# Hybrid decoder layer: weight splits put 200 places forward in the planner's priorities, and the memory tiles of the values asked for two at a time

## The chip, the cores and the metric

The kernel runs on one core of a Trainium2 chip. A core has a matrix engine (TensorE, PE in the profile; its weight loads are PEld), a vector engine (VectorE, DVE), a scalar engine (ScalarE, ACT), GpSimd (POOL) and a queue engine (SyncE, SP), and 16 DMA engines that all queues share. SBUF is the working memory, PSUM holds the sums that TensorE makes. The metric is the time of one execution in microseconds (us), as the device gives it; the median of three runs is compared.

## The reference

One layer on 512 tokens of width 1024, everything in float32:

```python
x = x + 0.5 * swiglu(rms_norm(x, norm_ffn1_w), ffn1_w_in, ffn1_w_out)        # d_ff 2816
x = x + hybrid_mixer(rms_norm(x, norm_mix_w), ...)    # 16 SSD heads, 8 differential-attention heads
x = x + memory_cross_attention(rms_norm(x, norm_cross_w), rms_norm(mem, norm_mem_w), w_cq, w_ck, w_cv, w_co)
x = x + 0.5 * swiglu(rms_norm(x, norm_ffn2_w), ffn2_w_in, ffn2_w_out)
out = rms_norm(x, norm_final_w)
```

The part that the change touches by name is the values of the cross-attention, `v = rms_norm(mem, norm_mem_w) @ w_cv`, with `mem` of 256 rows of width 1024. The other part, the way a weight is made ready, concerns nearly every matrix between the first feed-forward block and the second.

## The kernel before

**Splits.** A float32 product is made of three fast products: each operand is split into a high part (an ACT copy into a shorter format, `wh`, `hmh`, ...) and a low part (DVE: the operand less the high part, `wl`, `hml`, ...), and TensorE computes high x high, high x low, low x high. `split_into` (L152 to L161) issues the pair, the ACT instruction first and the DVE instruction that needs its result second. For weights, `load_w` (L172 to L181) takes one of six raw buffers (`wr`), asks for it on SP, takes one of three pairs `wh`, `wl`, and splits: 1.06 us on ACT and 1.23 us on DVE for a tile of 128x1024. Weight n + 3 gets the pair of weight n when the last product that reads weight n is done, so at most two weights can be ready ahead of the one that TensorE works on. One weight tile feeds 24 products of 512 columns, 5.4 us of TensorE. The quads of both feed-forward blocks (`raw_w`, `split_w`) and the last matrix (`out_blocks`) have splits of their own, which the change does not touch.

**Who decides the order.** Python generators write the program down in one long list. `Order` keeps a clock `t` that each written matmul moves on by its estimated time (520 columns at 2400 a microsecond, 0.22 us), a list of dense generators (projections) and a list of spawned chains, each with the time at which its next step is due. So the chains' small steps are written between the matmuls of the projections. For SP and POOL the written order is the order of execution (`manual_schedule`). For TensorE, ACT and DVE a planner goes over the list ahead of time: whenever an engine is free in its estimate, it takes the ready instruction with the lowest priority number, and that number is the place in the list. What comes out is one fixed order for each engine; on the chip an engine runs its instructions in this order and waits where an operand is not there. A weight's split is written with its `load_w`, that is when the product before it has been written completely; it gets ahead of work written earlier only where that work is not ready.

**The memory tiles.** `mem` is needed three times: for its norm, for the keys (`hm`) and for the values (`hm2`). `memory_prep` (L966 to L972) asks for the eight tiles of 128x256 at once on SP, with `memory_tile` (L952 to L955), then splits one every 3.0 us of the planner's clock into `hm2` (ACT L159, DVE L160), each placed behind the latest weight's split (`behind(recent)`). The call for the values is in `group_dense(3)` (L813 to L824): the chain starts 1.0 us after the first of the group's four tiles of `wxbc` has begun. A memory tile takes one of 16 small buffers (tag `s1`), which hold the group chains' small tiles (`xde`, `st`) too.

**The surroundings.** `group_dense(g)` makes the four convolved tiles of SSD group g (`xbc_tile`: a projection, then `conv` on ACT L805 and three DVE steps L808, `th` L796 and L797), then two gate tiles (`wz`). The chain `group(g)` (L838 to L947) runs beside the projections that follow: small transposes and products, `st` states (L878 to L886), the decay rows (ACT L899 to L902, DVE L903), `py`, then the norm. `decays` (L829 to L836) brings the decay rows of the next group from DRAM through ACT's own DMA queue into the tiles `gate` and `th` (L835); ACT issues them when the products that read the earlier rows are done. After group 3 come the last three tiles of the attention's output projection (`out_attn`, `pm`, L786), the values of the memory (`memory_values`, `pcv`, weights `wcv`), and the output projection of the SSD part.

Of the kernel before, what the change touches and what calls it, by code (L numbers as in the profile page):

```python
# [20 lines left out]
KT = D // P  # L21
# [18 lines left out]
W |= {"c0": 4.97, "cs": 3.0, "ct": 4.82}  # L40

SPLIT, AHEAD = 5, 2
MASKED = 8e30

B11, B12, B21, B22 = range(4)
# [3 lines left out]
C_FFN1, C_MIX, C_CROSS, C_MEM, C_FFN2, C_SSD = (8 * i for i in range(6))  # L49
# [51 lines left out]
def body(tc, a, dbg=None):  # L101
# [13 lines left out]
    def nm(s):  # L115
        uid[0] += 1
        return f"{s}_{uid[0]}"

    def s2(s, dt=F32, shape=(P, T)):
        if math.prod(shape[1:]) <= T // 2:  # L120
            return sp.tile(list(shape), dt, tag="s1", name=nm(s), bufs=NHALF)
        return sp.tile(list(shape), dt, tag="s2", name=nm(s))
# [7 lines left out]
    def acc(s, shape=(P, T)):  # L130
        return acc_p.tile(list(shape), F32, tag="acc", name=nm(s))
# [10 lines left out]
    od = Order()  # L142
# [9 lines left out]
    def split_into(hi, lo, src, scale=None):  # L152
        if scale is None:
            return (
                S.activation(hi, src, AF.Copy),  # L155
                V.tensor_tensor(lo, src, hi.bitcast(F32), ALU.subtract),  # L156
            )
        return (
            S.activation(hi, src, AF.Copy, scale=scale),  # L159
            V.scalar_tensor_tensor(lo, src, scale, hi.bitcast(F32), ALU.mult, ALU.subtract),  # L160
        )  # L161

    def split(s, src, scale=None, half=False, n=T):
        if half:
            both = s2(s, R32, (P, 2, T // 2))
            hi, lo = both[:, 0], both[:, 1]
        else:
            hi, lo = s2(s + "h", R32, (P, n)), s2(s + "l", R32, (P, n))
        last[:] = [i.ins for i in split_into(hi, lo, src, scale)]
        return hi, lo  # L170

    def load_w(src, n=D):  # L172
        raw = wp.tile([P, n], F32, tag="wr", name=nm("wr"), bufs=6)
        nc.sync.dma_start(raw, src)
        hi = wp.tile([P, n], R32, tag="wh", name=nm("wh"))
        lo = wp.tile([P, n], R32, tag="wl", name=nm("wl"))
        with ExitStack() as after:
            for i in start:
                after.enter_context(tc.issue_after(i))
            recent[:] = [i.ins for i in split_into(hi, lo, raw)]  # L180
        return hi, lo  # L181

    @contextmanager
    def behind(ins):
        with ExitStack() as after:
            for i in ins:
                after.enter_context(tc.issue_after(i))
            yield
# [129 lines left out]
    def proj(ps, w, xs, ks=None):  # L318
        n = len(xs)
        for k in ks or range(n):  # L320
            mm3(ps, w, xs[k], k == 0, k == n - 1, wc=slice(k * P, (k + 1) * P))
            yield


    par = cp.tile([P, NPAR], F32, name="par")
# [154 lines left out]
    def ffn1(h, wa, on_final, at_out):  # L480
        row4, xs = None, []
        wq, plain = iter(a["f1q"]), a["f1i"]
        for ti, (_, nf) in enumerate(THIRDS):
            g = []
            nq = nf // 2
            if ti == 0:
                for made in ffn_first(h, wa):
                    if made is None:
                        yield
                    else:  # L490
                        g.append(split("g", gated(*made, st1.row)))
                row4 = s2("row4")
                V.tensor_scalar(row4, st1.row, 0.5, None, ALU.mult)
                for n in range(NPLAIN - 2):
                    xs.append(block_sums(2 * n, C_FFN1, of_halves(h[2 * n], h[2 * n + 1])))
                    pg, pu = acc("pg"), acc("pu")
                    yield from proj(pg, load_w(plain[n][0]), h)
                    yield from proj(pu, load_w(plain[n][1]), h)
                    g.append(split("g", gated(pg, pu, st1.row)))
                nq -= NPLAIN // 2  # L500
            yield from ffn_quads(xs, wq, st1, nq, whole_tiles(g), BY_TILE)
            at_out(ti)
            for o in range(KT):
                po = acc("po")
                yield from proj(po, load_w(a[f"f1o{ti}"][o], nf * P), g)
                upd = s2("upd")
                V.tensor_tensor(upd, po, row4, ALU.mult)  # L507
                V.tensor_tensor(x[o], x[o], upd, ALU.add)
                if ti == len(THIRDS) - 1:
                    on_final(o)  # L510
# [12 lines left out]
    def beside(ti):  # L523
        if ti == 1:
            od.spawn(prepare())
            od.spawn(memory_norm())
        elif ti == 2:
            od.spawn(memory_prep(hm))
# [17 lines left out]
    def prepare():  # L546
# [19 lines left out]
        rel_far = s2("rel_far", shape=(8, RW - T))  # L566
        V.memset(rel_far, MASKED)
        nc.gpsimd.dma_start(rel_d[:, T:], rel_far)
# [224 lines left out]
    def silu2(src):  # L793

        th = s2("th2")
        S.activation(th, src, AF.Tanh, scale=0.5)  # L796
        V.scalar_tensor_tensor(th, th, 1.0, src, ALU.add, ALU.mult)  # L797
        return th

    def xbc_tile(n, dst):  # L800
        ps = acc("pxbc")
        yield from proj(ps, load_w(a["wxbc"][n]), h)
        y = s2("conv")
        cw = C_CONVW + 4 * n
        S.activation(y, ps, AF.Identity, bias=par[:, C_CONVB + n : C_CONVB + n + 1], scale=par[:, cw + 3 : cw + 4])  # L805
        for j in (2, 1, 0):
            d = 3 - j
            V.scalar_tensor_tensor(y[:, d:], ps[:, : T - d], par[:, cw + j : cw + j + 1], y[:, d:], ALU.mult, ALU.add)  # L808
        dst.append(silu2(y))
# [3 lines left out]
    def group_dense(g):  # L813
        bc, xs, zs = [], [], []
        if g == 3:
            od.spawn(memory_prep(hm2, 3.0), 1.0)
        yield from xbc_tile(8 + g, bc)
        yield from xbc_tile(12 + g, bc)
        for j in range(2):
            yield from xbc_tile(2 * g + j, xs)  # L820
        od.spawn(group(g, bc[0], bc[1], xs, zs), W["g0"])
        for j in range(2):
            ps = acc("pz")
            yield from proj(ps, load_w(a["wz"][2 * g + j]), h)  # L824
            zs.append(silu2(ps))
# [126 lines left out]
    def memory_tile(k):  # L952
        mk = s2("mem", shape=(P, MEM))
        nc.sync.dma_start(mk, a["memT"][k])
        return mk  # L955
# [7 lines left out]
        yield 3.0  # L963
        yield from st_mem.finish(42.0)

    def memory_prep(dst, apart=2.0):  # L966
        mem = [memory_tile(k) for k in range(KT)]
        for k, mk in enumerate(mem):
            with behind(recent):
                dst.append(split("hm", mk, par[:, C_MEM + k : C_MEM + k + 1], True))  # L970
            yield apart

    def memory_keys():
# [67 lines left out]
    hm, hm2 = [], []  # L1041
# [4 lines left out]
    for hd in range(1, 4):  # L1046
        od.add(queries_keys(hd))
    od.add(group_dense(0))
    od.add(out_attn(0, 0, 8))
    od.add(values(1))  # L1050
    for hd in range(4, 8):
        od.add(queries_keys(hd))
    od.add(group_dense(1))
    od.add(out_attn(1, 0, SPLIT))
    od.add(group_dense(2))
    od.add(group_dense(3))
    od.add(out_attn(1, SPLIT, 8, True))
# [352 lines left out]
```

## Time and profile before

| | |
|---|---|
| median of three runs | 1330.36 us (1329.17 to 1332.38) |
| profiled execution | 1330.36 us |
| its span, first to last instruction | 1328.6 us |
| mean granted TensorE clock | 0.995 |
| TensorE busy | 1307.6 us, 98% of the span |
| DVE busy | 946.4 us, 71% |
| ACT busy | 667.5 us, 50% |
| POOL busy | 114.1 us, 9% |

The profile has one row per group of instructions, wait or issue. In a timeline a row has the start and the duration in us from the beginning of the span, the engine (a q behind it marks the engine's queue, which issues transfers), the line of the kernel, the operation, what it writes and reads, the number of merged instructions, and in brackets how long the engine sat idle before it and what ended that. A row of the waits names who waited for whom, with the total, the number of times and the longest. TensorE's matmuls overlap: one that lasts 0.39 us starts 0.23 us after the one before it when TensorE runs freely. So time lost on TensorE is read from the starts: the distance of two starts less 0.23 us.

### The profile page before, as it was taken

Reading aid. Unit: us, or ns where it says so; the run is one execution under the profiler, and the core shown is the slowest. Engines: PE = TensorE matmul, PEld = TensorE weight load, DVE = VectorE, ACT = ScalarE, POOL = GpSimd, SP = SyncE. Lnnn points to the kernel's source line nnn. Section 1 sums busy time; section 2 is a strip of 40 time slices with the busy share of each in tenths; the row PEclk is TensorE's granted clock in tenths of the full one; section 3 lists DMA queues with packets and bytes.
Section 4 is the critical chain, followed back from the end, with each engine's and each line's share of the span. In section 5 each row is a group of like instructions: output and inputs, shape, how many; then the busy total and the mean of one; then the engine's idle time right before and its main releaser. Section 6 shows DMA issues by size and latency. Waiting matters only on the chain.

```text
span 1328.6 us, 19969 instructions
## 1 busy us (share of the span) xinstructions
PE 1307.6 (98%) x7767; PEld 1137.1 (86%) x7767; DVE 946.4 (71%) x1498; ACT 667.5 (50%) x1116; POOL 114.1 (9%) x127
## 2 busy tenths in 40 slices
PE   9999999999999999999999999999999999999997
PEld 7898998899887778777888777888889999989995
DVE  6874778477786586557867677645688877877886
ACT  6442445154454565346545456434455645554564
POOL 0000010000020111100012021120001100000001
PEclk9999999999999999999999899999999999999999
DMA  7444577555583734673365757675138976666662
GB/s 271 112 126 127 125 203 246 132 146 172 189 251 89 212 73 105 185 241 88 88 186 128 192 138 221 196 192 165 62 114 227 250 228 176 191 195 179 188 201 94
DMA packets 74143, 222.71 MB, mean 168 GB/s; under 512 B 8424, under 2 KB 20176, under 8 KB 73696
## 3 DMA queue, kind: packets, MB, share of 16 engines
q1 hardware_dynamic: 52400, 174.42, 39.1%
q0 software_dynamic: 11904, 40.45, 16.8%
q10 hardware_dynamic: 9744, 6.56, 2.4%
q8 instruction: 61, 1.00, 0.3%
q14 instruction: 34, 0.28, 0.1%
HBM read 219.24 MB, written 50.91 MB: 203 GB/s over the span
## 4 chain that ended last, share of the span: by engine, by line
PE 93%; DVE 3%; ACT 2%; issue 1%; POOL 1%; DMA 0%; POOLq 0%; SPq 0%; ACTq 0%; DVEq 0%
PE qb L240 12%; PE po L146 10%; PE pm L146 9%; PE qe L240 8%; PE qa L240 8%; PE pxbc L146 7%; PE pk L146 3%; PE pq L146 3%; PE pcq L146 3%; PE pv L146 3%; PE pz L146 3%; PE ob L1195 3%; PE oa L1195 2%; PE oe L1195 2%; PE pa L146 2%; PE pg L146 2%
## 5 line engine op out<-in xcount | busy, mean ns | idle before, releaser
L155 ACT ACTIVATE wh<-wr 128x1024 fp32r<-128x1024 f32 (+2 forms) x311 | 316.7, 1021 | 391.9 <-issue 60.8
L156 DVE TENSOR_TENSOR wl<-wr,wh 128x1024 fp32r<-128x1024 f32 (+2 forms) x311 | 366.0, 1179 | 133.0 <-ACT wh L155 126.1
L146 PE MATMUL po<-gl,wh 128*128 128x512 f32 x176 | 68.5, 390 | 0.0
L146 PE MATMUL po<-gh,wh 128*128 128x512 f32 x176 | 68.4, 391 | 0.0
L146 PE MATMUL po<-gh,wl 128*128 128x512 f32 x176 | 68.4, 389 | 0.0
L240 PE MATMUL qa<-hml,wh 128*128 128x256 f32 x216 | 61.1, 283 | 0.0
L240 PE MATMUL qa<-hmh,wl 128*128 128x256 f32 x216 | 61.1, 283 | 0.0
L240 PE MATMUL qa<-hmh,wh 128*128 128x256 f32 x216 | 61.1, 283 | 0.0
L146 PE MATMUL pxbc<-hnh,wh 128*128 128x512 f32 x128 | 53.3, 416 | 1.8 <-ACT wh L155 1.8
L146 PE MATMUL pxbc<-hnh,wl 128*128 128x512 f32 x128 | 51.5, 402 | 0.8 <-DVE wl L156 0.8
L146 PE MATMUL pxbc<-hnl,wh 128*128 128x512 f32 x128 | 51.3, 401 | 0.0
L709 ACT ACTIVATE ec<-ec,mn 128x512 f32<-128x512 f32 (+3 forms) x64 | 35.4, 555 | 23.8 <-DVE mn L708 23.8
L507 DVE TENSOR_TENSOR upd<-po,row 128x512 f32<-128x512 f32 x24 | 16.6, 690 | 39.4 <-PE po L146 39.2
L240 PE MATMUL qe<-s31h,wl 128*128 128x256 f32 x152 | 43.2, 284 | 0.5 <-DVE wl L156 0.5
L240 PE MATMUL qb<-s24h,wl 128*128 128x256 f32 x152 | 43.1, 284 | 0.5 <-DVE wl L156 0.5
L240 PE MATMUL qe<-s31h,wh 128*128 128x256 f32 x152 | 43.1, 284 | 0.0
L240 PE MATMUL qe<-s24h,wh 128*128 128x256 f32 x152 | 43.0, 283 | 0.0
L240 PE MATMUL qb<-s31h,wl 128*128 128x256 f32 x152 | 43.0, 283 | 0.0
L240 PE MATMUL qb<-hmh,wh 128*128 128x256 f32 x152 | 43.0, 283 | 0.0
L240 PE MATMUL qb<-hml,wh 128*128 128x256 f32 x152 | 43.0, 283 | 0.0
L240 PE MATMUL qb<-hmh,wl 128*128 128x256 f32 x152 | 43.0, 283 | 0.0
L240 PE MATMUL qe<-s24h,wl 128*128 128x256 f32 x152 | 43.0, 283 | 0.0
(444 smaller groups left out, 4036.8 us busy)
## 6 DMA issues: line engine op xcount, KB each, us to landing
wr<-in_f2q SPq DMA_DIRECT2D x44, 512.0 KB, 4.4
wr<-in_f1q SPq DMA_DIRECT2D x40, 512.0 KB, 4.4
isum<-in_f2q SPq DMA_DIRECT2D x22, 512.0 KB, 6.0
wr<-isum SPq DMA_DIRECT2D x22, 512.0 KB, 4.3
wsum<-in_f2b SPq DMA_DIRECT2D x20, 512.0 KB, 8.4
wr<-wsum SPq DMA_DIRECT2D x20, 512.0 KB, 4.6
wr<-in_f1q POOLq DMA_DIRECT2D x16, 512.0 KB, 5.6
wr<-in_f1o SPq DMA_DIRECT2D x16, 512.0 KB, 3.8
```

Source lines behind the costliest of these rows:

```text
L146: newest_mm[:] = [nc.tensor.matmul(out, w, x, start=start, stop=stop).ins]
L155: S.activation(hi, src, AF.Copy),
L156: V.tensor_tensor(lo, src, hi.bitcast(F32), ALU.subtract),
L240: newest_mm[:] = [nc.tensor.matmul(out, a_[:, wc], b_, start=first and f == 0 and kp == 0 and j == 0, stop=kp == n - 1 and j == 2, skip_gr ...
L507: V.tensor_tensor(upd, po, row4, ALU.mult)
L709: S.activation(ec[:, :n], ec[:, :n], AF.Exp, bias=mn, scale=-1.0, accum_out=sm[c][:, i : i + 1])
L1195: newest_mm[:] = [nc.tensor.matmul(ps, a_[:, ts], b_[:, ws], start=first and k == 0 and j == 0, stop=k == n - 1 and j == 2, skip_group_che ...
```

## The change

`load_w` writes the two instructions of its split under a priority that is 200 places lower in number, so the planner treats them as if they had been written 200 places earlier in the list. The DMA that fetches the weight is outside of this, and SP's order does not depend on priorities. Which instructions exist is not changed.

`memory_prep` gets a parameter `ahead`, the number of tiles asked for before the first split. Its default is all eight, which keeps the call for the keys as it is. The call for the values passes 2: two tiles at the start, and then, ahead of split k, tile k + 2. So the first step of the chain writes three requests, each of the next five steps one, 3.0 us of the planner's clock apart, and the last two none.

```diff
 SPLIT, AHEAD = 5, 2
+EARLY = 200
...
         with ExitStack() as after:
             for i in start:
                 after.enter_context(tc.issue_after(i))
+            after.enter_context(tc.high_priority(offset=EARLY))
             recent[:] = [i.ins for i in split_into(hi, lo, raw)]
         return hi, lo
...
         if g == 3:
-            od.spawn(memory_prep(hm2, 3.0), 1.0)
+            od.spawn(memory_prep(hm2, 3.0, 2), 1.0)
...
-    def memory_prep(dst, apart=2.0):
-        mem = [memory_tile(k) for k in range(KT)]
-        for k, mk in enumerate(mem):
+    def memory_prep(dst, apart=2.0, ahead=KT):
+        mem = [memory_tile(k) for k in range(ahead)]
+        for k in range(KT):
+            if k + ahead < KT:
+                mem.append(memory_tile(k + ahead))
             with behind(recent):
-                dst.append(split("hm", mk, par[:, C_MEM + k : C_MEM + k + 1], True))
+                dst.append(split("hm", mem[k], par[:, C_MEM + k : C_MEM + k + 1], True))
             yield apart
```

## The prediction

> **What bounds the kernel now.** I read the page first, then TensorE's waits, then timelines of each engine around the longest of these waits.
>
> ```profile
> span 1328.6 us, 19969 instructions
> PE 1307.6 (98%) x7767; PEld 1137.1 (86%) x7767; DVE 946.4 (71%) x1498; ACT 667.5 (50%) x1116; POOL 114.1 (9%) x127
> ```
>
> TensorE is busy for 98% of the span, and neither edit removes a matmul. So nothing can be gained but what TensorE loses by waiting, 1328.6 - 1307.6 = 21.0 us of idle time, and what a slower clock costs. TensorE's waits (total, times, longest) show where:
>
> ```profile
> PE pxbc L146 <- ACT wh L155: 1.8, 1, 1.8
> PE nrow L146 <- POOL ndiag L368: 1.1, 1, 1.1
> PE pm L146 <- DVE x L786: 0.9, 1, 0.9
> PE pxbc L146 <- DVE wl L156: 0.8, 1, 0.8
> PE pv L146 <- ACT wh L155: 0.6, 1, 0.6
> ```
>
> Three of these five are waits for a weight's split (`wh`, `wl`): two at one `pxbc` tile, one at `pv`. Here is TensorE at that tile:
>
> ```profile
> 742.64 0.39 PE L146 MATMUL pxbc<-hnh,wl 128*128 128x512 f32 x1
> 744.84 0.51 PE L146 MATMUL pxbc<-hnh,wh 128*128 128x512 f32 x1 [1.81 <-ACT wh L155]
> 745.18 0.60 PE L146 MATMUL pxbc<-hnl,wh 128*128 128x512 f32 x1
> 746.59 0.79 PE L146 MATMUL pxbc<-hnh,wl 128*128 128x512 f32 x1 [0.82 <-DVE wl L156]
> 747.19 0.63 PE L146 MATMUL pxbc<-hnh,wh 128*128 128x512 f32 x1
> ...
> 751.88 0.47 PE L146 MATMUL pxbc<-hnh,wl 128*128 128x512 f32 x1
> 752.19 0.40 PE L146 MATMUL pxbc<-hnh,wh 128*128 128x512 f32 x1
> ```
>
> From 742.64 to 752.19 there are 16 starts in 9.55 us. At 0.23 us each (751.88 and 752.19 are still wider; the rows at 796 below have 0.23) they would take 3.65, so 5.9 us are lost here. Two waits make 3.15 of it: 744.84 - 742.64 - 0.23 = 1.97, and 746.59 - 745.18 - 0.23 = 1.18. The other 2.7 are rate: from 747.19 to 751.88 eleven matmuls start 0.43 us apart. It is the clock, by the stretch's own row (busy time of PE, PEld, DVE, ACT and POOL, then the granted clock, 0.66, the DMA share and the rate):
>
> ```profile
> 742.00:752.00 10.00, 7.37 (x20) 5.07 (x19) 8.23 (x12) 6.10 (x10) 0.00 (x0) 0.66 0.69 210
> ```
>
> Why was the weight late? Not for its transfer. The queue of SP, what the issue at 722.34 took to land, and the fixed order on ACT and on DVE:
>
> ```profile
> 692.63 29.07 SPq L954 DMA_DIRECT2D mem<-in_memT  x8
> 722.34 1.01 SPq L174 DMA_DIRECT2D wr<-in_wxbc  x2
> ```
>
> ```profile
> wr<-in_wxbc SPq DMA_DIRECT2D x1, 512.0 KB, 7.5
> ```
>
> ```profile
> 742.04 0.49 ACT L159 ACTIVATE hm<-mem,par 128x256 fp32r<-128x256 f32 x1
> 742.44 0.61 ACT L902 ACTIVATE gate<-gate 128x512 f32<-128x512 f32 x1
> 743.06 0.78 ACT L805 ACTIVATE conv<-pxbc,par 128x512 f32<-128x512 f32 x1
> 743.74 1.99 ACT L155 ACTIVATE wh<-wr 128x1024 fp32r<-128x1024 f32 x2
> ```
>
> ```profile
> 743.88 1.53 DVE L808 SCALAR_TENSOR_TENSOR conv<-pxbc,par,conv 128x511 f32<-128x511 f32 x2
> 745.33 1.21 DVE L156 TENSOR_TENSOR wl<-wr,wh 128x1024 fp32r<-128x1024 f32 x1
> ```
>
> The weight landed 7.5 us after 722.34, at 729.8, and was split only at 743.74. On ACT the `conv` of the tile before stands in front of it, which can't start until TensorE is through with that tile. So TensorE ends a tile, waits for `conv`, then for `wh`, and two matmuls later for `wl`, which stands behind two `conv` steps on DVE. The planner writes such an order when the weight comes late in its own estimate, and on SP eight memory tiles stand in front of the request; the chip, too, spent 29.07 us on them. SP's waits say what held them:
>
> ```profile
> SPq L954 <- DMA th<-cum_d: 12.4, 2, 6.5
> SPq L954 <- DMA gate<-cum_d: 10.9, 2, 7.7
> ```
>
> Four of the eight went out only when one of ACT's four transfers of decay rows had landed, 23.3 us together. The tiles weren't urgent: the first `hm` of this group starts 44 us after the first request.
>
> ```profile
> L159 ACT ACTIVATE hm<-mem,par x8: 492/492/501, 736.8 to 782.9; 128x256 fp32r<-128x256 f32 x8
> ```
>
> **The change part by part.** *Memory tiles two at a time.* No transfer is added or removed: eight issues of about 0.33 us move on SP, and weights pass some of them. The chain's steps are 3.0 us of the planner's clock apart and the weights 5.2 (24 x 0.22); the first step comes 1.0 to 1.3 us into the first tile. So the late weight is written 3.9 us after that step, behind four memory tiles (three, then one) and not eight, the next one behind six, the third behind seven. SP's waits don't vanish: if they go by the count of transfers, they now fall on the fourth tile, on the late weight, and on the fifth and sixth tiles. The weight would go out after the two `gate` waits, 29.07 - 12.4 = 16.7 us into the stretch, at about 709 and not at 722.34. That is 13 us more of lead for a weight that had 14 to spare, so by itself it buys nothing on the chip; it counts through the planner's order. POOL's queue is neither passed nor moved. The `hm` splits come at the same steps as before, each 6 us after its request; the 7.5 us above are more than that, so ACT could wait for one in order, up to 1.5 us. I cost this at nothing: the `wh` behind it has two tiles of lead, 10.9 us, and if that cover is gone it costs those 1.5.
>
> *The 200 places.* A projection writes 24 matmuls and a dozen other instructions, so 200 places are about five projections, and a ready split goes in front of any `conv`, decay or `x` step. The three pairs still bound it: it can't run more than two tiles ahead. Most splits gain nothing, as ACT already idles until TensorE frees the pair, as in this row:
>
> ```profile
> ACT wh L155 <- PE po L146: 58.1, 16, 4.9
> ```
>
> Where it does bite, the work passed is held up by 1.0 us on ACT (two splits in the 1.99 above) and 1.21 on DVE. Queued behind are `conv`, the decay steps and the `x` updates; TensorE waits for these through `py`, `pcb` and the PSUM banks, and other matmuls cover it as long as there are any.
>
> *Both at 744.* Three places for the split are thinkable. Ahead of the decay steps: it ends before 742.87, when TensorE wants it, and all 5.9 us are saved. Behind `hm`, in place of the decay step at 742.44: it runs from about 742.5 to 743.6 and TensorE goes on 0.06 later (as 744.84 follows 743.74 and 1.04), 0.8 lost; `wl` runs to 744.85, and the third matmul starts at 744.9 and not at 744.1, another 0.8: 4.3 saved. Behind `conv` as now: only `wl` passes two DVE steps, about 0.5 saved. I take 4.3: in the planner's estimate the request still leaves late, since it stands behind four memory tiles, and the place behind `hm` is the nearest to today's that lies ahead of `conv`. Both ends are kept.
>
> Would 1.6 us of waits still cost clock? In proportion to this stretch, 2.7 for 3.15, they would cost 1.3, and 3.0 were saved. The row of the nearest size says no: behind 1.09 us of idle time the matmuls start 0.23 apart.
>
> ```profile
> 796.46 0.50 PE L146 MATMUL nrow<-ndiag,ones_r 128*128 128x512 f32 x1 [1.09 <-POOL ndiag L368]
> 796.80 0.40 PE L146 MATMUL pcv<-wh,hm 128*128 128x512 f32 x1
> 797.03 0.39 PE L146 MATMUL pcv<-wl,hm 128*128 128x512 f32 x1
> ```
>
> The Trainium skill, page TensorE: Matmul & The Clock Gate, section on the HAM clock gate, states that the array falls to half clock after about 3.4 us without work and comes back after about as long of work, in windows that run freely. By that rule 1.6 us of waits cost no clock and 4.3 us are saved; by the proportion 3.0. The trace agrees roughly: 3.15 us of waits with two matmuls between them, then about 5 us at 0.43.
>
> *At `pv`.* TensorE goes from `pm` to the first weight of the values and waits for its split, which stands behind a decay step on ACT:
>
> ```profile
> 544.48 0.96 PE L146 MATMUL pv<-wh,hnh 128*128 128x512 f32 x3 [0.64 <-ACT wh L155]
> ```
>
> ```profile
> 542.87 0.61 ACT L902 ACTIVATE th<-th 128x512 f32<-128x512 f32 x1
> 543.39 1.99 ACT L155 ACTIVATE wh<-wr 128x1024 fp32r<-128x1024 f32 x2
> ```
>
> Without that step `wh` ends 0.5 to 0.6 us sooner, and the two splits before it can move as well: I take the whole wait and its restart, 0.64 and 0.16, as 0.8 (bounds 0 and 0.8).
>
> The sum: 4.3 + 0.8 = 5.1 us. The profiled execution took 1330.36 us (span 1328.6 and 1.8 around it), which is the median of the three runs too, so the forecast is 1330.36 - 5.1 = 1325.3 us. The other waits of the list, 1.1 at `nrow` and 0.9 at `pm`, are for POOL and DVE; I leave them as they are.
>
> **The rivals.** *The split stays behind `conv`.* If the weight's estimated landing is still later than `conv` can start, the split isn't ready when the priority would help, and the change doesn't do what it says. Then 0.5 + 0.8 = 1.3 us are saved, or none: 1329.1 to 1330.4. For it: four tiles still stand in front and SP's waits remain. Against it: four fewer, and on the chip the weight had landed 14 us before.
>
> *The weights' splits hold up DVE, slower.* After group 3's tiles DVE is nearly full, and TensorE waits for it twice:
>
> ```profile
> 787.09 0.68 DVE L786 TENSOR_TENSOR x<-x,pm 128x512 f32<-128x512 f32 x1
> 788.35 1.22 DVE L156 TENSOR_TENSOR wl<-wr,wh 128x1024 fp32r<-128x1024 f32 x1
> 794.23 0.15 DVE L364 TENSOR_TENSOR cl<-rh,ch 128x4 f32<-128x4 f32 x1
> 794.30 1.21 DVE L156 TENSOR_TENSOR wl<-wr,wh 128x1024 fp32r<-128x1024 f32 x1
> ```
>
> `x` frees a PSUM bank for `pm`, and `cl` goes through POOL's `ndiag` into `nrow`. Both stand right ahead of a `wl` now; the 200 places let `wl` pass. With two splits in front of each, both waits grow by 2 x 1.21, 4.8 us together, and at 3.3 and 3.5 us each they reach the length that cost 2.7 us of clock at 744: 4.8 + 5.4 = 10.2 lost against 5.1 gained, 1335.5. It decides from 7.8 us of loss on (5.1 and the 2.7 that are 0.2%). Against it: a split needs a free pair, one per 5 us, so two in front of the same step are rare.
>
> *All of it goes.* The split stands ahead of the decay steps, and the earlier weights let DVE and POOL catch up: 5.9 + 0.8 + 1.1 + 0.9 = 8.7 us, 1321.7.
>
> **How the numbers follow.** The forecast has 0.44, with a range of its own from 6.7 us saved (5.9 + 0.8) to 3.0 (the clock lost in proportion, nothing at `pv`), 1323.7 to 1327.4. All of it has 0.12, no effect 0.22, slower 0.22. About 0.2%, 2.7 us, is what a measurement of this kernel can tell from no change; so faster is 0.44 + 0.12 = 0.56, same 0.22, slower 0.22. The range goes from the full gain, 1321.5, to 1333.0, where slower begins; beyond it lies most of the slower case and little else.
>
> **What would show it.** In the profile after, SP's memory tiles no longer stand in one row of 29 us, and a `wxbc` request lies between them at about 709. On ACT the `wh` of that tile stands ahead of the `conv` of the tile before. TensorE's waits for `wh` and `wl` at `pxbc` fall from 1.8 and 0.8 to under 1 each, the wait at `pv` is gone, and the clock of the stretch is 1.00. The prediction is wrong if `conv` still precedes `wh`, if the waits for `x` and `ndiag` grow past 2 us, or if a new wait of TensorE stands where a decay or `conv` step was passed.

## The result, and the profile after

The changed kernel takes 1337.01 us, median of 4 runs (1336.37 to 1337.68), against 1329.94 us for the kernel before in 4 runs: 1.0050 times as long, with a 95% interval from 1.0033 to 1.0067. The forecast was 1325.3, and the result lies beyond the range's upper end, 1333.0. The profiled execution took 1336.96 us.

The page of the changed kernel, span and first row of the busy times:

```profile
span 1335.2 us, 19980 instructions
...
PE 1310.4 (98%) x7767; PEld 1139.0 (85%) x7767; DVE 946.9 (71%) x1498; ACT 667.9 (50%) x1116; POOL 111.8 (8%) x127
```

The span has grown by 6.6 us, and TensorE still runs for 98% of it. TensorE's waits in the changed kernel (total, times, longest; a line of the kernel now has a number higher by one or two):

```profile
PE pn L147 <- POOL ysq L933: 4.5, 2, 4.0
...
PE pxbc L147 <- ACT wh L156: 2.3, 1, 2.3
PE nps L147 <- DVE nacc L388: 1.1, 2, 0.8
...
PE pm L147 <- DVE x L788: 0.9, 1, 0.9
PE pxbc L147 <- DVE wl L157: 0.6, 1, 0.6
```

The wait at the second `pxbc` tile is still there. The wait at `pv` is gone, and so is POOL's `ndiag`. At the head stands a new one: 4.0 us at `pn`, the norm of group 3. TensorE's timeline there:

```profile
824.02 0.39 PE L147 MATMUL pcv<-wh,hm 128*128 128x512 f32 x1
828.39 1.86 PE L147 MATMUL pn<-ones,ysq 128*128 128x1 f32 x8 [3.98 <-POOL ysq L933]
830.12 0.77 PE L147 MATMUL pm<-ysh,wh 128*128 128x512 f32 x1
830.69 0.63 PE L147 MATMUL pm<-ysl,wh 128*128 128x512 f32 x1
831.12 0.63 PE L147 MATMUL pm<-ysh,wl 128*128 128x512 f32 x1
```

The same place in the kernel before:

```profile
824.87 1.05 PE L146 MATMUL pn<-ones,ysq 128*128 128x1 f32 x8 [0.23 <-POOL ysq L931]
```

Behind the wait the matmuls start 0.43 us apart and not 0.23. The granted clock of the stretch 825 to 840 (the seventh figure: behind the times of the five engines) in the changed kernel:

```profile
825.00:840.00 15.00, 11.61 (x41) 9.70 (x42) 5.51 (x10) 3.59 (x6) 7.46 (x7) 0.77 0.77 178
```

and in the kernel before:

```profile
825.00:840.00 15.00, 15.00 (x70) 12.20 (x71) 8.78 (x15) 5.66 (x9) 6.42 (x6) 1.00 0.74 183
```

From the starts of TensorE's matmuls, as in the prediction, the difference of the two executions is made of: at `pn` +3.8 (4.14 against 0.39), slow rate behind it +3.1 (the eight small products of `pn` and the 22 matmuls behind them take 9.1 us and not 6.0), at the second `pxbc` tile +0.4 (its two waits 3.5 against 3.2), at `nps` in the first feed-forward block +0.9, two small ones at 203 and 647 us +0.9; and -0.8 at `pv`, -1.45 at `nrow` near 796. Together about +6.9, and -0.3 in smaller places.

What makes `pn` late stands on ACT. The changed kernel:

```profile
811.29 0.61 ACT L901 ACTIVATE e<-th 64x512 f32<-64x512 f32 x1
814.36 1.06 ACT L156 ACTIVATE wh<-wr 128x1024 fp32r<-128x1024 f32 x1 [2.46 <-PE pcv L147]
815.33 1.27 ACT L903 ACTIVATE th<-th,cum 128x128 f32<-128x128 f32 x4
...
817.28 1.06 ACT L156 ACTIVATE wh<-wr 128x1024 fp32r<-128x1024 f32 x1
818.24 0.62 ACT L904 ACTIVATE th<-th 128x512 f32<-128x512 f32 x1
818.76 1.27 ACT L903 ACTIVATE th<-th,cum 128x128 f32<-128x128 f32 x4
...
823.76 2.00 ACT L156 ACTIVATE wh<-wr 128x1024 fp32r<-128x1024 f32 x2 [2.54 <-PE pcv L147]
825.67 0.61 ACT L931 ACTIVATE ysq<-y 128x512 f32<-128x512 f32 x1
```

The kernel before, the same decay steps and the same square:

```profile
809.51 1.57 ACT L901 ACTIVATE th<-th,cum 128x128 f32<-128x128 f32 x5
...
811.51 0.97 ACT L901 ACTIVATE th<-th,cum 128x128 f32<-128x128 f32 x3
812.39 1.04 ACT L155 ACTIVATE wh<-wr 128x1024 fp32r<-128x1024 f32 x1
...
822.81 0.63 ACT L929 ACTIVATE ysq<-y 128x512 f32<-128x512 f32 x1 [3.24 <-DVE y L927]
```

Two things have changed places. Before, three of the values' last five splits stood ahead of the eight `th` steps; these were done by 812.5, and the other two splits followed. Now all five stand ahead. ACT comes to the first `e` step of the `th` rows 3 us later (811.29 and not 808.23), and then it sits idle for 2.46 us until TensorE frees the pair of the fifth split, with the eight decay steps behind it; they end at about 820. And before, the second square ran as soon as `y` was there. Now two splits of the output projection stand in front of it; their pairs come free only with the last products of the values, at 823.76, so the square ends at 826.28. By then TensorE has nothing left but `pn`.

The start of `pn` is 3.5 us later than in the kernel before, and the rows of DVE, ACT and POOL say what that is made of. DVE has the second `y` ready at 824.93 (824.24 and 0.69) and not at 822.78: 2.15, the decay steps' part. The square starts 0.74 behind it and not 0.03: 0.7, the two splits' part (ACT's 2.54 us of idle time in front of them end before `y` is there). POOL's sum of squares takes 1.92 and not 1.29: 0.6, to which the last section comes back.

SP did what the prediction worked out: the second weight is asked for at 708.73 behind four memory tiles, and the waits for ACT's decay rows fall on the fourth tile, on the weight, and on the fifth and sixth.

```profile
693.53 1.68 SPq L956 DMA_DIRECT2D mem<-in_memT  x3
...
705.29 0.34 SPq L956 DMA_DIRECT2D mem<-in_memT  x1
708.73 0.33 SPq L175 DMA_DIRECT2D wr<-in_wxbc  x1
717.03 7.22 SPq L956 DMA_DIRECT2D mem<-in_memT  x2
```

But ACT's order at that tile is the old one, `conv` first:

```profile
744.46 0.76 ACT L807 ACTIVATE conv<-pxbc,par 128x512 f32<-128x512 f32 x1
745.12 1.99 ACT L156 ACTIVATE wh<-wr 128x1024 fp32r<-128x1024 f32 x2
```

### The profile page after: what moved, and what is told of

Its sections match the earlier page's. It is cut to its first block, busy times and chain, and to the rows that moved or that the text cites. A ratio compares the mean times of both kernels' runs of the same rounds, so it can differ in the third digit from the quotient of the medians.

```text
span 1335.2 us, 19980 instructions
## 1 busy us (share of the span) xinstructions
PE 1310.4 (98%) x7767; PEld 1139.0 (85%) x7767; DVE 946.9 (71%) x1498; ACT 667.9 (50%) x1116; POOL 111.8 (8%) x127
## 4 chain that ended last, share of the span: by engine, by line
PE 88%; DVE 4%; issue 3%; ACT 2%; DMA 1%; POOL 1%; SPq 0%; POOLq 0%; DVEq 0%; ACTq 0%
PE qb L242 12%; PE po L147 10%; PE pm L147 10%; PE qe L242 8%; PE qa L242 7%; PE pxbc L147 6%; PE pk L147 3%; PE pq L147 3%; PE pcq L147 3%; PE pv L147 3%; PE pz L147 3%; PE ob L1199 3%; PE oa L1199 2%; PE oe L1199 2%; PE pg L147 2%
## 5 line engine op out<-in xcount | busy, mean ns | idle before, releaser
L242 PE MATMUL qb<-s24h,wh 128*128 128x256 f32 x152 | 43.0, 283 | 0.0
```

The source lines that it names most:

```text
L242: newest_mm[:] = [nc.tensor.matmul(out, a_[:, wc], b_, start=first and f == 0 and kp == 0 and j == 0, stop=kp == n - 1 and j == 2, skip_gr ...
```

## The experiments

Each median stands beside that of the kernel before on the same chip; "tile" and "pn" are what TensorE lost in waits of over 0.38 us, from its starts in the profiled execution, at the second `wxbc` tile of group 3 (735 to 757 us) and between the values and the output projection (815 to 840). In the kernel before they are 3.2 and 0.4.

| run | us | before | ratio (95%) | tile | pn |
|---|---|---|---|---|---|
| the change | 1337.01 | 1329.94 | 1.0050 (1.0033 to 1.0067) | 3.5 | 4.1 |
| e1_priority_only | 1335.06 | 1330.59 | 1.0039 (1.0025 to 1.0053) | 3.2 | 4.1 |
| e2_memory_only | 1329.45 | 1330.59 | 0.9999 (0.9990 to 1.0009) | 3.4 | 0.4 |
| e3_values_own_place | 1330.98 | 1330.59 | 1.0005 (0.9996 to 1.0014) | 3.7 | 0 |
| e4_out_own_place | 1335.95 | 1330.59 | 1.0044 (1.0029 to 1.0059) | 3.7 | 4.3 |
| e5_tiles_later | 1321.98 | 1328.92 | 0.9947 (0.9930 to 0.9963) | 0 | 0 |
| e6_tiles_later_values_own | 1321.60 | 1328.92 | 0.9944 (0.9929 to 0.9959) | 0 | 0 |
| e7_tiles_later_all | 1328.78 | 1328.92 | 0.9998 (0.9989 to 1.0007) | 0 | 4.2 |
| e8_60_places | 1329.08 | 1328.92 | 0.9998 (0.9989 to 1.0008) | 3.6 | 0 |
| e9_after_square | 1337.97 | 1329.30 | 1.0067 (1.0051 to 1.0084) | 3.7 | 6.1 |
| e10_later_after_square | 1328.80 | 1329.30 | 0.9995 (0.9986 to 1.0004) | 0 | 5.3 |
| e11_after_cvh | 1333.84 | 1329.04 | 1.0034 (1.0022 to 1.0046) | 3.7 | 2.8 |
| e12_later_after_cvh | 1324.99 | 1329.04 | 0.9966 (0.9951 to 0.9980) | 0 | 1.8 |

**Which half of the change.** The first run keeps only the 200 places, the second only the memory tiles.

```diff
-            od.spawn(memory_prep(hm2, 3.0, 2), 1.0)
+            od.spawn(memory_prep(hm2, 3.0), 1.0)
```

> Only the 200 places; the memory tiles are asked for eight at once, as before. Theory (the 200 places lose it in the values' stage, where the splits of the values' weights now stand on ACT in front of the decay steps of group 3, wait there for a pair, 2.46 and 2.54 us, and make the end of the chain late): the wait of TensorE for the squares at `pn` stays at about 4 us with about 2.4 us of half clock behind it, and the time is that of the changed kernel, 1336 to 1338 us. Rival (the memory tiles between the weights on SP lose it): the wait at `pn` is under 1 us and the time is 1326 to 1331.

```diff
-            after.enter_context(tc.high_priority(offset=EARLY))
```

> Only the memory tiles two at a time; every split keeps its own place. Theory (the 200 places lose it): as the kernel before, 1329 to 1331 us, with the wait of 1.45 us at `nrow` near 796 back, no wait over 1 us at `pn`, and the late split of the second `wxbc` tile of group 3 still behind `conv`. Rival (the memory tiles lose it): 1335 to 1338.

The 200 places alone lose: 1335.06 with the whole wait at `pn`, a little under the 1336 expected. The memory tiles alone make no difference (1329.45), and the late split stays where it was. The two don't add up to the change in full: the 200 places are 4.5 us over their kernel before, the change is 7.1 over its own, and where the rest comes from is shown only for the profiled executions. The first run's profiled execution shows one thing more. Its waits at the second `pxbc` tile are those of the kernel before to a hundredth (1.97 and 1.19 from the starts), but no slow clock follows:

```profile
745.52 0.50 PE L147 MATMUL pxbc<-hnh,wh 128*128 128x512 f32 x1 [1.81 <-ACT wh L156]
745.86 0.40 PE L147 MATMUL pxbc<-hnl,wh 128*128 128x512 f32 x1
747.28 0.50 PE L147 MATMUL pxbc<-hnh,wl 128*128 128x512 f32 x1 [1.02 <-DVE wl L157]
747.62 0.39 PE L147 MATMUL pxbc<-hnh,wh 128*128 128x512 f32 x1
747.85 0.40 PE L147 MATMUL pxbc<-hnl,wh 128*128 128x512 f32 x1
```

The thirteen matmuls behind the second wait take 3.1 us here and 5.5 in the changed kernel's profiled execution. So 2.4 us of the difference between these two (1333.81, the lowest of its five, and 1336.96) is slow rate that here didn't come.

**Which weights.** The third run lets the eight values' weights keep their own place, the fourth those of the output projection.

```diff
-    def load_w(src, n=D):
+    def load_w(src, n=D, early=True):
...
-            after.enter_context(tc.high_priority(offset=EARLY))
+            if early:
+                after.enter_context(tc.high_priority(offset=EARLY))
...
-            w = wcv[k] if k < len(wcv) else load_w(a["wcv"][k])
+            w = wcv[k] if k < len(wcv) else load_w(a["wcv"][k], early=False)
```

The third run has this at all three places that load `wcv`. The fourth has instead, in `out_proj`:

```diff
-        ws = [load_w(wts[o]) for o in range(ahead)]
+        ws = [load_w(wts[o], early=src is not ys) for o in range(ahead)]
...
-            yield from proj(po, load_w(wts[o]), src)
+            yield from proj(po, load_w(wts[o], early=src is not ys), src)
```

> The whole change, but the eight weights of the values (`wcv`) keep their own place in the list; all others go 200 places forward. Theory (these eight, in front of the decay steps, are the cause): the wait at `pn` falls from 4.0 to under 1 us, the half clock behind it is gone (6.2 us together), the 1.45 us at `nrow` may come back: 1330.8 to 1332.2 us. Rival (the two splits of the output projection that stand between the two squares on ACT are the cause): they are still ahead of the `cvh` steps, the wait stays at 3 us or more, 1335 to 1338.

> The whole change, but the weights of the output projection (`wos`) keep their own place. On ACT only the first of them moves back, behind all but one of the last decay steps; the values' splits still stand in front of the decay steps. Theory (the values' splits are the cause): about one split (1.06 us) and its wait less in front of the decay steps, so the wait at `pn` is 2 to 4 us and the time 1333 to 1337. Rival (the output projection's splits are the cause): the wait is under 1 us, 1330 to 1332.

With the values' weights at their own place `pn` doesn't wait and the time is 1330.98, as the theory said. In the fourth run the wait stays, 3.5 us, and the time is 1335.95, inside the theory's range. I read this as "the values' splits, and they alone". That was too much: in the third run the two splits of the output projection stand behind the second square as well (825.79 and 824.06 on ACT), and in the fourth they still stand ahead of it (823.87 and 825.78). Neither run had told the two apart. The seventh showed it.

**The late split at the second tile.** One number of the kernel before is changed, the time at which the memory tiles' chain begins; the sixth run adds the whole change, without the values' weights, the seventh adds all of it.

```diff
-            od.spawn(memory_prep(hm2, 3.0), 1.0)
+            od.spawn(memory_prep(hm2, 3.0), 18.0)
```

> The kernel before, with one number changed: the chain of the values' memory tiles starts 18.0 us of the planner's clock after the group's first tile has begun, not 1.0; all eight tiles are still asked for at once and no split has another priority. Theory (the second `wxbc` weight of group 3 is split late because its request is written behind the memory tiles, which wait for small buffers in the planner's estimate): its split stands ahead of `conv`, the 5.9 us lost at this tile are gone, and the time is 1330.5 - 5.9 = 1324.6, between 1323.5 and 1326. Rival (the split can't get ahead of `conv` without a priority of its own, or the stall only moves to the tiles behind): 1329 to 1331.

> The whole change with the eight values' weights at their own place (the run that gave 1330.98) and the chain of the memory tiles 18.0 us after the tile and not 1.0. Theory: the loss at the second `wxbc` tile goes as with the kernel before, and the 200 places still save the wait at `pv`: 5.9 + 0.8 less than 1330.5, 1323.8, between 1322.5 and 1325.5. Rival (the 200 places cost as much elsewhere as they save at `pv`): 1325 to 1327, no better than the later tiles alone.

> The whole change, values' weights too 200 places forward, and the chain of the memory tiles 18.0 us after the tile and not 1.0. On ACT two splits stand among the last four decay steps of group 3 and their `th` steps. Theory (a split in front of decay steps waits for its pair with them behind it): the wait at `pn` is there again, 1 to 4 us with or without slow clock behind it, 1325 to 1331. Rival (the stall at `pn` came only of the disturbed tile at 744 and what followed it): no wait over 0.5 at `pn`, 1323 to 1325.

This one number is worth 6.9 us: 1321.98 against 1328.92, more than was expected, as the wait of 1.45 us at `nrow` falls to 0.5 and that for `x` is gone too. SP now asks for two more `wxbc` weights ahead of the memory tiles:

```profile
696.55 9.46 SPq L174 DMA_DIRECT2D wr<-in_wxbc  x2
...
706.67 20.37 SPq L954 DMA_DIRECT2D mem<-in_memT  x8
```

ACT splits the weight of the second tile as soon as a pair is free, at 729.52, and TensorE is busy without a gap at full clock (the row of 736 to 756):

```profile
729.52 1.06 ACT L155 ACTIVATE wh<-wr 128x1024 fp32r<-128x1024 f32 x1 [0.35 <-PE pz L146]
```

```profile
736.00:756.00 20.00, 20.00 (x105) 16.56 (x104) 15.15 (x23) 11.97 (x23) 0.00 (x0) 1.00 0.68 210
```

So the split needed no priority; it needed its request to be written ahead of the memory tiles. The run moves the chain as a whole, its `hm` steps too; but by the planner's rule these were not what stood in the way, since with 200 places the split is ranked ahead of them, and it stayed behind `conv`. In the sixth run the 200 places add nothing to this that can be measured (1321.60): the rival's reading, though the time is below both ranges. It is the fastest kernel here, 0.9944 of the kernel before.

The seventh run gives 7 us back, and its ACT shows the second cause most plainly. The decay steps are done by 810.4, and `y` is ready at 815.68, but ACT, idle for 4.49 us until the pairs come free, makes two splits at 815.42 before it takes the square, 1.7 us behind `y`:

```profile
810.32 0.62 ACT L931 ACTIVATE ysq<-y 128x512 f32<-128x512 f32 x1
815.42 2.00 ACT L156 ACTIVATE wh<-wr 128x1024 fp32r<-128x1024 f32 x2 [4.49 <-PE pcv L147]
817.34 0.61 ACT L931 ACTIVATE ysq<-y 128x512 f32<-128x512 f32 x1
```

**How many places.** The whole change with 60 places.

```diff
-EARLY = 200
+EARLY = 60
```

> The whole change with 60 places in place of 200. In the values' stage the splits then stand behind the decay steps again, nearly as before. Theory: no wait over 1 us at `pn`, the stall at 744 stays, 1329.5 to 1331.5. Rival (splits put forward lose it by however few places): 1334 to 1338.

1329.08, a little under the theory's range, and by its mechanism: the last decay steps are ahead of the next split again and `pn` doesn't wait. The wait at `pv` is gone here too. So the loss isn't in putting splits forward, but in putting them past the decay steps and the square.

**The two causes apart.** The next two runs hold the second and third split of the output projection behind the second square, with the tiles early and late.

```diff
-            for i in start:
+            for i in (*start, *then):
...
-            S.activation(q_, yz[j], AF.Square)
+            squares[:] = [S.activation(q_, yz[j], AF.Square).ins]
...
-        ws = [load_w(wts[o]) for o in range(ahead)]
+        ws = [load_w(wts[o], then=squares if src is ys and o else ()) for o in range(ahead)]
...
-            yield from proj(po, load_w(wts[o]), src)
+            yield from proj(po, load_w(wts[o], then=squares if src is ys and o == ahead else ()), src)
```

> The whole change, but on ACT the second and the third split of the output projection stand behind the second square of group 3, not ahead of it; the eight values' splits still stand in front of the decay steps. Theory (most of the loss is the decay steps' lateness, the two splits add the rest): the second `y` is ready at about 825 as in the changed kernel, the square and POOL's sum take 0.6 and 1.3 to 2.0 us from there, and TensorE waits at `pn` for 2.7 to 3.3 us instead of 4.1; with the half clock kept or gone, 1333 to 1336.3. Rival (the two splits ahead of the square are all of it): the wait is under 1 us, 1330 to 1332.

> The kernel of the run before last with later tiles and all splits forward (1328.78, a wait of 4.0 us at `pn`), with the same two splits behind the second square. There `y` was ready at 815.7, as the last product of the values went out. Theory: the square and POOL's sum still follow it, 1.7 to 2.4 us of wait at `pn`, 1324.5 to 1327 as the half clock goes or stays. Rival (the two splits are all of it): under 0.7 us, 1321.5 to 1323.5.

The waits at `pn` came out as the theory said, 2.8 and 1.8 us, and the times did not: 1337.97 and 1328.80, nothing gained. TensorE's waits and DVE's order in the first of the two show where it went:

```profile
PE pm L147 <- DVE cvl L161: 3.2, 1, 3.2
PE pn L147 <- POOL ysq L933: 3.2, 2, 2.6
```

```profile
827.39 2.36 DVE L157 TENSOR_TENSOR wl<-wr,wh 128x1024 fp32r<-128x1024 f32 x2
829.67 2.72 DVE L161 SCALAR_TENSOR_TENSOR cvl<-pcv,ncol,cvh 128x512 fp32r<-128x512 f32 x4
```

The two splits now stand in front of `cvl`, which reads the values out of PSUM and frees the bank for `pm`. Moved behind one thing that TensorE needs, they stand in front of the next. In the kernel before a `cvh` and its `cvl` came first. The last two runs restore that (shown against the run before; the line of `proj` changes in the same way, and the squares are no longer kept):

```diff
             cv[tb].append(split("cv", pv[tb][n], st_mem.col[:, tb : tb + 1]))
+            first[:] = first or last
...
-        ws = [load_w(wts[o], then=squares if src is ys and o else ()) for o in range(ahead)]
+        ws = [load_w(wts[o], then=first if src is ys and o else ()) for o in range(ahead)]
```

> The whole change, but the second and the third split of the output projection stand behind the second square and behind the first `cvh` and `cvl` step (which frees a PSUM bank for `pm`); the values' splits still stand in front of the decay steps. Theory (two causes: the decay steps' lateness, and two splits that stand in front of what TensorE needs next): the 3.3 us at `pm` of the run before are gone, the 2.8 us at `pn` stay, 1338.0 - 3.3 = 1334.6, or 1332.9 if the half clock behind it goes too; 1332.5 to 1335.2. Rival (only the two splits matter): the wait at `pn` is under 1 us, 1330 to 1331.5.

> The same with the memory tiles' chain 18.0 us after the tile. Theory (two causes): the 3.4 us at `pm` are gone, the 1.8 us at `pn` stay, 1328.8 - 3.4 = 1325.4, or 1323.6 without the half clock; 1323.3 to 1325.8. Rival (only the two splits matter): 1321.5 to 1322.8, as fast as with the values' weights at their own place.

Both times lie where the two-cause theory put them, 1333.84 and 1324.99. So both causes are real. With late tiles the two splits cost 3.8 us (1328.78 to 1324.99) and the late decay steps 3.4 (1324.99 to 1321.60). With early tiles, beside their own kernels before: 1337.01 is 7.1 over, 1333.84 is 4.8 over, 1330.98 is 0.4 over; that is 2.3 for the two splits and 4.4 for the decay steps. By the 95% intervals each of these sizes can be off by 2 to 3 us. That both are there doesn't hang on them: with late tiles the single times of the three kernels don't overlap, and the waits at `pn` alone are 4.1, 2.8 and 0 with early tiles, 4.2, 1.8 and 0 with late ones.

## Why the prediction was wrong

**The bound and the stall were read rightly.** TensorE's waits are what the time is made of, and the 5.9 us at the second `wxbc` tile can be had: moving the memory tiles out of the way saved 6.9 with what followed from it.

**The memory tiles: the step on SP was right, and costing it at nothing too.** The request went out at 708.73 (forecast: about 709), the waits fell on the tiles named, and the edit alone made no difference.

**"Both at 744" failed: 4.3 us forecast, nothing saved.** The step chose the place behind `hm` because it was the nearest to today's that lies ahead of `conv`. The split stayed behind `conv`, as the first rival had it. A priority only chooses among instructions that the planner holds to be ready, and behind four memory tiles the split was still not ready in its estimate. The same paragraph says that the request "still leaves late"; from that the rival followed, not the forecast. That the place of the request among the memory tiles is the cause, the fifth run shows; what in the planner's estimate holds the memory tiles back so long (buffers or the waits for ACT's transfers) was not tried.

**`pv` was right**: the wait is gone, 0.80 us. But in this execution splits put forward cost 1.4 us elsewhere: 0.9 where they go in front of the `nacc` steps that `nps` needs, 0.4 where one goes in front of an attention step at 647. The first of these differs from run to run (0.4 in the first, none in the third, 1.6 in the seventh). By the times nothing is left of the gain: with the values' weights excepted, the change takes 1330.98, the memory tiles alone 1329.45.

**"Other matmuls cover it as long as there are any" is the step that cost most.** The price of passed work was put at 1.0 us on ACT and 1.21 on DVE for each split. What was left out is that a split put forward can also wait for its pair, and all behind it waits too: 2.46 and 2.54 us in the changed kernel, 4.49 in the seventh run, up to four times the work of one split. (The 2.54 and the 4.49 were over before `y` was there. What they cost is that the two splits' own 2.0 us then fell in front of the square, which came 0.7 and 1.7 us late.) And the cover was assumed for the whole kernel, though at one place it ends: `pn` follows directly on the last product of the values, so there the lateness of the decay steps, the squares and the `cvl` comes out as time of TensorE. The sum had no term for this place, and it measured 3.8 us of wait and 3.1 of slow rate. Under "What would show it" the prediction does name both failures as signs of being wrong: `conv` still ahead of `wh`, and a new wait where a decay step was passed. It gave the second no price.

**The slower rival had the right sign and nearly the right time (1335.5), for another reason.** It had DVE held up at `x` and `ndiag`. Both are no worse: `x` still 0.9 us, `ndiag` gone. Of what it says, only the slow clock behind a longer wait came true, at another place.

**The clock.** The step said that 1.6 us of waits cost no clock, from the row with 1.09 us. The runs don't allow so firm a line; see the last section.

## What to carry to other kernels

An instruction put forward in an order that is fixed ahead of time takes its own wait with it: on an engine that works in order, everything behind it waits for its buffer as well. So before work is put forward, find for each place the point where the cover ends, that is where the last product that doesn't depend on the passed work runs out, and keep what that point needs (here the decay steps, the square, the read-out of PSUM) ahead. And where a step is late because its input is asked for late, move the request: one changed number on the side of the requests gave what 200 places of priority on the side of the work did not.

## What was not expected of the hardware

**Equal waits, unequal clock.** At the second `pxbc` tile the kernel before and the first run have the same two waits, 1.97 and 1.19 us from the starts. The thirteen matmuls behind them take 5.6 us in the one and 3.1 in the other: 2.5 us of slow rate, or nothing. The row of 736 to 757 in the kernel before and in the first run:

```profile
736.00:757.00 21.00, 18.37 (x70) 14.17 (x69) 13.26 (x21) 13.25 (x26) 0.00 (x0) 0.84 0.73 210
```

```profile
736.00:757.00 21.00, 18.17 (x93) 14.45 (x92) 15.72 (x25) 13.70 (x26) 0.00 (x0) 1.00 0.83 231
```

The executions of the kernel before fit that. Of the 63 beside the experiments the 16 that took under 1328.4 us have a granted clock of 0.998, all others 0.995 to 0.997.

And in the last run a single wait of 1.68 us was enough, with a delay. The eight small products of `pn` and four matmuls near full rate follow it, and only then eight that start 0.39 to 0.43 us apart (granted clock 0.51 from 820 to 823.5).

```profile
818.04 1.05 PE L147 MATMUL pn<-ones,ysq 128*128 128x1 f32 x8 [1.68 <-POOL ysq L933]
...
819.74 0.39 PE L147 MATMUL pm<-ysh,wh 128*128 128x512 f32 x1
819.96 0.59 PE L147 MATMUL pm<-ysl,wh 128*128 128x512 f32 x1
820.35 0.63 PE L147 MATMUL pm<-ysh,wl 128*128 128x512 f32 x1
```

The Trainium skill, page TensorE: Matmul & The Clock Gate, section on the HAM clock gate, says that the activity windows run freely, about 3.4 us each, and that the clock falls after at least one idle window. The free run agrees with equal waits that end differently; a whole idle window does not agree with 1.68 us, nor with the 2.7 us that it is if the small products of `pn` (1.05 us) don't count as work, which no run here tells. The measurement decides: in these runs waits of 1.7 to 4.1 us cost 1.4 to 3.1 us more, or nothing.

**POOL beside DVE.** The sum of squares on POOL took 1.26 us in the ninth run, with DVE idle, and 1.92 us in the changed kernel. There the second of two `wl` subtractions was running on DVE when it started, and POOL ended 1.1 us after that one:

```profile
824.91 1.26 POOL L933 TENSOR_TENSOR ysq<-ysq,ysq 128x512 f32<-128x512 f32 x1 [30.36 <-issue]
```

```profile
826.42 1.92 POOL L933 TENSOR_TENSOR ysq<-ysq,ysq 128x512 f32<-128x512 f32 x1 [31.05 <-issue]
```

In the fourth run POOL came first, 0.03 us ahead of the second `wl`. POOL took 1.26 us, and DVE's two subtractions 3.45 and not the 2.36 that they take in the changed kernel:

```profile
825.43 3.45 DVE L157 TENSOR_TENSOR wl<-wr,wh 128x1024 fp32r<-128x1024 f32 x2
```

```profile
826.53 1.26 POOL L934 TENSOR_TENSOR ysq<-ysq,ysq 128x512 f32<-128x512 f32 x1 [31.07 <-issue]
```

The Trainium skill, page SBUF — State Buffer, section on the two separate sides, says that a DVE instruction with two SBUF inputs and a GpSimd instruction that reads SBUF exclude each other on a shared pair of ports, and that whichever starts first holds it for its whole length. Both cases agree. So splits moved to this chain put 0.6 to 0.7 us more on it, or are held up themselves. Spans on POOL are rough, but the same 1.92 and 1.97 us stand in the first and the seventh run, where a `wl` was running too.
